# The first MLP product of a diffusion backbone by seven block products for eight

## The chip, the cores and the metric

The kernel runs on one core of a Trainium2 chip. Time is device microseconds of one execution; the number that counts is the median of several. Engine names are those of the profile: PE is TensorE (PEld its weight loads), DVE is VectorE, ACT is ScalarE, POOL is GpSimd, and SP is SyncE, which here only issues DMAs. A name with a q (SPq) is the queue of instructions of that engine. Each engine works its own queue off in order, so an instruction that waits holds up what stands behind it in that queue.

## The reference, cut to what matters

The kernel computes one layer of a hybrid backbone for 512 latent and 128 context tokens (640 in all, D = 1024), in float32. Ahead of the MLP lie an input projection, four token mixers (pooling, Fourier, RWKV-7, gated linear attention), a gated merge and an output projection. The part that the change is about:

```python
h = _rmsnorm(xf, p['norm2_g']) * (1.0 + sc2) + sh2
ff = jnp.einsum('blf,fd->bld', jnp.square(jax.nn.relu(jnp.einsum('bld,df->blf', h, p['mlp_w1']))), p['mlp_w2'])
xf = xf + g2 * ff
```

`mlp_w1` is 1024 x 4096 and `mlp_w2` 4096 x 1024. A final RMSNorm follows.

## The kernel before, in words

Every float32 matrix is split into two parts, a rounded high part (`fp32r`) and the rest. A product is then three products: high by high, high by low, low by high. The split of a weight tile is `load` (L249): a DMA of 128x512 numbers into one of three `wr` buffers (`fetch`, L238 to L242), a cast on ACT (L246) and a subtraction on DVE (L247).

Up to some 180 us the program loads the inputs, makes the modulation vectors from `ada_w` (`araw`, `acc`: DVE), and starts the input projection (`proj`, L368). Then come the two RWKV halves (`hp` = 0 and 1, from L686 on). Each needs masks made by POOL: `G.affine_select` on the tiles `ab` and `sl` (L780, 24 of them for each half), after which SP writes `ab` to DRAM as `adr` (L785) and reads it back. Between these dependent pieces PE does tiles of the input projection, which need only weights. From 521 us on come the linear attention, the gated merge and the output projection (L1240), then the MLP.

The order of the instructions on each engine is not the order of the source. A scheduler sets it: each engine gets what it believes ready, by priority (`tc.high_priority` raises it), and the order is then fixed. Ordering between engines is by semaphores.

The MLP works in four groups of 1024 hidden features. `hidden` (L1349 to L1361) makes 128 features by 320 tokens (half of the 640, `HN`): eight k-tiles by three terms, 24 matmuls of 320 columns (L1354), then the squared ReLU and the split into `fh` and `fl`. A group has 16 of these, 384 matmuls; the four together have 1536. The group then multiplies by its rows of `mlp_w2`, 240 matmuls of 512 columns (L1400), and adds the result to the residual `xf`, which stays in the fast memory of the core. The last half of the last group is L1420, with the final norm behind it. The normalised input is transposed by PE (`transposed`, L1319 to L1332) into `nh` and `nl`; that of the last 128 tokens is done inside the first `hidden` tiles.

Of the kernel before, what the change touches and what calls it, by code (L numbers as in the profile page):

```python
# [10 lines left out]
F32 = mybir.dt.float32  # L11
# [8 lines left out]
P = 128  # L20
# [45 lines left out]
def laid_out(x):  # L66
# [6 lines left out]
        "t_w1": blocks(x["mlp_w1"][0], range(0, FF, P), P),  # L73
# [63 lines left out]
def backbone(ctx, tc, a, y_prompt, y_sample, out_rwkv, out_gla):  # L137
# [484 lines left out]

    def split_into(y, j, src):
        S.copy(y[0][:, j, :], src)
        V.tensor_tensor(y[1][:, j, :], src, f32(y[0][:, j, :]), ALU.subtract)
# [60 lines left out]
    for hp in range(2):  # L686
# [221 lines left out]
        for step in range(8):  # L908
            live = [(0, 0, step), (1, 1, 2 + step)] + ([(2, 0, 8 + step), (3, 1, step)] if step < 2 else [])
# [139 lines left out]
    for n in range(7):  # L1049
        p = 64 >> n  # L1050
# [225 lines left out]
    nh = h2.tile([P, KT, NT], F32R, name="nh")  # L1276
    nl = h2.tile([P, KT, NT], F32R, name="nl")
# [16 lines left out]
    def projected(i, hf, acc, t):  # L1294
# [7 lines left out]
        S.activation(t[:, bs], xf[i][:, bs], AF.Square, accum_out=ss[:, 2 * i + hf : 2 * i + hf + 1])  # L1302

# [14 lines left out]

    def transposed(i, t):  # L1319
        c = i // 4  # L1320
        sl_ = slice(i * P, i * P + P)
        for k4 in range(2):
# [4 lines left out]
            for k in range(4):  # L1327
                kk = k4 * 4 + k
                S.activation(tm[:, k], pt[:, k * P : k * P + P], AF.Identity, scale=s2[:, kk, c : c + 1], bias=b2[:, kk, c : c + 1])
            ks = slice(k4 * 4, k4 * 4 + 4)  # L1330
            S.copy(nh[:, ks, sl_], tm)
            V.tensor_tensor(nl[:, ks, sl_], tm, f32(nh[:, ks, sl_]), ALU.subtract)  # L1332
# [14 lines left out]
    with tc.tile_pool(name="mlp", bufs=1, reuse_waits="tile") as mp, \  # L1347
            tc.tile_pool(name="pf2", bufs=5, space=PSUM, reuse_waits="tile") as pf2:
        def hidden(w, h, l, b):  # L1349
            pt = pbank()  # L1350
            bs = slice(b * HN, b * HN + HN)
            for k in range(KT):
                for n, (wk, m) in enumerate(((w[0], nh), (w[0], nl), (w[1], nh))):
                    PE.matmul(pt[:, :HN], lhsT=wk[:, k, :], rhs=m[:, k, bs], start=k == 0 and n == 0,  # L1354
                              stop=k == KT - 1 and n == 2)
            with hi():
                rl = mp.tile([P, HN], F32, name="rl", tag="rl", bufs=3)
                S.activation(rl, pt[:, :HN], AF.Relu)  # L1358
                V.tensor_tensor(rl, rl, pt[:, :HN], ALU.mult)  # L1359
                S.copy(h[:, bs], rl)  # L1360
                V.tensor_tensor(l[:, bs], rl, f32(h[:, bs]), ALU.subtract)  # L1361

        g2b = mp.tile([P, 2, D], F32, name="g2b")
        gf = mp.tile([P, D], F32, name="gf")
        NG = 4
        for g in range(NG):
            ws, fh, fl = [], [], []
            order = [(f, b) for f in range(8) for b in range(2)]
            if g == 0:
                order[:4] = [(0, 0), (1, 0), (0, 1), (1, 1)]  # L1370
            for f, b in order:
                if b == 0:
                    ws.append(load(a["t_w1"][g * 8 + f]))
                    fh.append(mp.tile([P, NT], F32R, name="fh", tag="fh", bufs=11))
                    fl.append(mp.tile([P, NT], F32R, name="fl", tag="fl", bufs=11))
                elif f == 0 and g == 0:
# [4 lines left out]
            if g == 0:  # L1381
# [81 lines left out]
```

## Time and profile before

| what | value |
|---|---|
| median of 3 runs | 1233.39 us (1231.15 to 1239.44) |
| the profiled execution | 1242.74 us, of which the span of instructions is 1241.0 us |
| mean granted clock in the profiled execution | 0.971 |
| PE busy | 1194.1 us, 96% |
| DVE busy / ACT busy / POOL busy | 734.0 / 500.5 / 61.8 us |
| moved by DMA | 147.41 MB, mean 119 GB/s |
| chain that ended last | PE 43%, of it L1354 18% and L1400 15% |

The page of the profile cuts the span into 40 slices of 31 us and gives for each the busy share of every engine in tenths, the granted TensorE clock, the busy share of the core's 16 DMA engines and the GB/s moved. The tables of stretches give the same for any piece of the span in numbers. Matmuls are pipelined, so the mean length of one (0.31 us) is longer than the time from one to the next; what counts is the length of a run of them divided by their number. The chain that ended last goes back from the last instruction, at each step to what released it. Idle time of an engine is put down to what ended it.

### The profile page before, as it was taken

How to read it: one execution, taken by the hardware profiler on the slowest of the kernel's cores; microseconds unless marked ns; L12 is line 12 of the kernel's file. 1: busy time of each engine (PE TensorE's matmuls, PEld its weight loads, DVE VectorE, ACT ScalarE, POOL GpSimd, SP SyncE). 2: the span in 40 equal slices, each digit the busy share in tenths (PEclk: the TensorE clock that was granted, in tenths of full speed). 3: DMA queues.
4: the chain of work that ended last, by engine and by line, in shares of the span. 5: the costliest groups of instructions: out<-in, count | busy, mean ns of one | idle time of the engine just before them, and what ended most of it. 6: DMA issues, size and time to landing. Idle time of an engine off the chain costs nothing.

```text
span 1241.0 us, 19640 instructions
## 1 busy us (share of the span) xinstructions
PE 1194.1 (96%) x7556; PEld 1032.8 (83%) x7556; DVE 734.0 (59%) x1458; ACT 500.5 (40%) x1024; POOL 61.8 (5%) x98
## 2 busy tenths in 40 slices
PE   7999999999998999998999989999999999999997
PEld 2778997889878798796578978998899899889985
DVE  4798767565479383446978746542453444245456
ACT  4732226542376522268535324532133124213432
POOL 0000001400114200200000000000000000000000
PEclk9999899799899699999999989999999999999998
DMA  9557652234214243153465550322222222222222
GB/s 353 207 173 256 219 182 79 74 97 118 84 48 123 59 124 101 58 172 99 150 216 159 190 197 28 100 69 83 70 78 76 79 74 75 79 78 76 69 93 85
DMA packets 85971, 147.41 MB, mean 119 GB/s; under 512 B 21693, under 2 KB 26206, under 8 KB 85878
## 3 DMA queue, kind: packets, MB, share of 16 engines
q1 hardware_dynamic: 85878, 146.16, 37.1%
q8 instruction: 59, 0.97, 0.3%
q14 instruction: 34, 0.28, 0.1%
HBM read 123.17 MB, written 22.95 MB: 118 GB/s over the span
## 4 chain that ended last, share of the span: by engine, by line
PE 43%; DMA 3%; DVE 3%; ACT 2%; issue 1%; DVEq 0%; ACTq 0%
PE pf L1354 18%; PE pf L1400 15%; PE po L1240 4%; PE pf L1420 2%; DMA wr<-in_t_out_dram 2%; PE px L1077 2%; DMA wr<-in_t_in_dram 1%; PE pt L368 1%; DVE acc L309 1%; DVE wl L247 0%; ACT eqm L1073 0%; PE pf L1325 0%; PE px L1151 0%; DVE gate L1202 0%; DMA mg<-mscr 0%
## 5 line engine op out<-in xcount | busy, mean ns | idle before, releaser
L247 DVE TENSOR_TENSOR wl<-wr,wh 128x512 fp32r<-128x512 f32 x222 | 151.4, 695 | 208.3 <-ACT wh L246 201.8
L246 ACT CAST wh<-wr 128x512 fp32r<-128x512 f32 x222 | 133.5, 618 | 345.3 <-PE pf L1400 139.1
L368 PE MATMUL pt<-xl,wh 128*128 128x320 f32 x816 | 202.0, 323 | 0.0
L368 PE MATMUL pt<-xh,wh 128*128 128x320 f32 x816 | 201.5, 324 | 0.2 <-DVE grow L337 0.2
L368 PE MATMUL pt<-xh,wl 128*128 128x320 f32 x816 | 198.1, 320 | 0.0
L1354 PE MATMUL pf<-nh,wl 128*128 128x320 f32 x512 | 158.1, 309 | 0.0
L1354 PE MATMUL pf<-nl,wh 128*128 128x320 f32 x512 | 157.9, 308 | 0.0
L1354 PE MATMUL pf<-nh,wh 128*128 128x320 f32 x512 | 157.8, 309 | 0.0
L368 PEld LDWEIGHTS pt<-xh,wh 128*128 128x128 f32 x816 | 140.1, 192 | 8.8 <-issue 4.0
L368 PEld LDWEIGHTS pt<-xl,wh 128*128 128x128 f32 x816 | 140.4, 192 | 7.7 <-issue 4.1
L368 PEld LDWEIGHTS pt<-xh,wl 128*128 128x128 f32 x816 | 139.9, 192 | 5.3 <-issue 2.2
L1400 PE MATMUL pf<-wl,fh 128*128 128x512 f32 x280 | 109.0, 389 | 0.0
L1400 PE MATMUL pf<-wh,fh 128*128 128x512 f32 x280 | 109.0, 389 | 0.0
L1400 PE MATMUL pf<-wh,fl 128*128 128x512 f32 x280 | 108.9, 389 | 0.0
L1354 PEld LDWEIGHTS pf<-nl,wh 128*128 128x128 f32 x512 | 96.0, 188 | 0.2
L1354 PEld LDWEIGHTS pf<-nh,wh 128*128 128x128 f32 x512 | 96.0, 188 | 0.1
L1354 PEld LDWEIGHTS pf<-nh,wl 128*128 128x128 f32 x512 | 96.0, 188 | 0.0
L309 DVE SCALAR_TENSOR_TENSOR acc<-araw,sc,acc 128x512 f32<-128x512 f32 x112 | 78.4, 744 | 12.5 <-DMA araw<-in_t_ada_dram 12.4
L1400 PEld LDWEIGHTS pf<-wh,fl 128*128 128x128 f32 x280 | 52.6, 188 | 11.0
L1400 PEld LDWEIGHTS pf<-wh,fh 128*128 128x128 f32 x280 | 52.5, 188 | 10.8
L1400 PEld LDWEIGHTS pf<-wl,fh 128*128 128x128 f32 x280 | 52.6, 188 | 10.8
L1359 DVE TENSOR_TENSOR rl<-rl,pf 128x320 f32<-128x320 f32 x64 | 30.9, 483 | 39.0 <-ACT rl L1358 39.0
(538 smaller groups left out, 1773.5 us busy)
## 6 DMA issues: line engine op xcount, KB each, us to landing
wr<-in_t_w_dram SPq DMA_DIRECT2D x128, 256.0 KB, 2.9
wr<-in_t_in_dram SPq DMA_DIRECT2D x102, 256.0 KB, 3.5
araw<-in_t_ada_dram SPq DMA_DIRECT2D x64, 256.0 KB, 3.7
adaw<-in_t_ada_dram SPq DMA_DIRECT2D x16, 512.0 KB, 9.3
mscr<-gate SPq DMA_DIRECT2D x24, 320.0 KB, 4.0
mg<-mscr SPq DMA_DIRECT2D x24, 320.0 KB, 4.0
uscr<-mg SPq DMA_DIRECT2D x15, 320.0 KB, 2.9
wr<-in_t_branch_dram SPq DMA_DIRECT2D x32, 128.0 KB, 2.2
```

What stands on the lines that cost most here:

```text
L246: S.copy(wh, raw)
L247: V.tensor_tensor(wl, raw, f32(wh), ALU.subtract)
L309: V.scalar_tensor_tensor(acc[j], raw, w, acc[j], ALU.mult, ALU.add)
L368: PE.matmul(pt[:, b, :HN], lhsT=w, rhs=m[:, b * HN : b * HN + HN], start=start and n == 0, stop=stop and n == 2)
L1077: PE.matmul(pt, lhsT=ek[:, ts_], rhs=em[:, :, ts_], start=True, stop=True)
L1240: PE.matmul(acc, lhsT=m[k][:, sl_], rhs=W[k, hf][w][:, 0, :], start=k == 0 and n == 0, stop=k == KT - 1 and n == 2)
L1354: PE.matmul(pt[:, :HN], lhsT=wk[:, k, :], rhs=m[:, k, bs], start=k == 0 and n == 0, stop=k == KT - 1 and n == 2)
L1359: V.tensor_tensor(rl, rl, pt[:, :HN], ALU.mult)
L1400: PE.matmul(acc[i], lhsT=m[k][:, ts_], rhs=w[:, kk, :], start=k == 0 and n == 0, stop=k == 7 and n == 2)
L1420: PE.matmul(acc, lhsT=m[k][:, ts_], rhs=ws[k][w][:, 0, :], start=k == 0 and n == 0, stop=k == 7 and n == 2)
```

## The change

The first MLP product is done on 2x2 blocks of both factors, with seven block products for eight (Strassen's scheme in Winograd's form). The input is cut by k (two halves of 512) and by tokens (two halves of 320), the weight by k and by 128 features: `t_w1` is stored in blocks of 512 rows by 128 features, 16 pairs of feature tiles. For each pair `pair_steps` does seven products of 12 matmuls of 320 columns (84 for a pair, 1344 in all) and forms the four results by additions on DVE and ACT from three banks.

Four of the seven products need sums of weight blocks. They are made in DRAM, in 16 buffers `wsum` of 1 MB (four sums for each of four groups): POOL issues 16 copying DMAs (DRAM to DRAM, `begin`) and 16 adding ones (`add`, which add their source onto the buffer). In the source `chore` places them in the RWKV loop. The sums of input blocks are made by `block_sums` on DVE and ACT after the last transposition. The residual goes to DRAM (`xres`) and comes back in the last group; `xf` collects the MLP output instead. The hidden tiles `fh` and `fl` have 8 buffers for 11.

```diff
-        "t_w1": blocks(x["mlp_w1"][0], range(0, FF, P), P),
+        "t_w1": np.ascontiguousarray(blocks(x["mlp_w1"][0], range(0, FF, P), P).reshape(16, 2, P, 2, 512).transpose(3, 1, 0, 2, 4)),
...
+    wsum = [[dpool.tile([4, P, 512], F32, name=f"wsum{n}_{g}") for g in range(4)] for n in range(4)]
+    w1b = a["t_w1"]
+    def sum_steps():
+        def rows(t):
+            return t.rearrange("j p c -> (j p) c")
+        def begin(n, g):
+            src = w1b[(0, 0, 1, 1)[n], (0, 1, 1, 0)[n], 4 * g : 4 * g + 4]
+            return lambda: nc.gpsimd.dma_start(out=rows(wsum[n][g]), in_=rows(src))
+        def add(n, g):
+            src = (w1b[0, 1, 4 * g : 4 * g + 4], w1b[1, 1, 4 * g : 4 * g + 4], wsum[0][g], wsum[2][g])[n]
+            return lambda: nc.gpsimd.dma_start(out=rows(wsum[n][g]), in_=rows(src), accum_op=ALU.add, max_dma_last_dim=8192)
+        steps = [begin(n, 0) for n in range(4)]
+        for g in range(4):
+            for n in range(4):
+                steps.append(add(n, g))
+                if g < 3:
+                    steps.append(begin(n, g + 1))
+        return steps
+    chores = sum_steps()
+    def chore(n):
+        for _ in range(min(n, len(chores))):
+            chores.pop(0)()
     def split_into(y, j, src):
...
         for step in range(8):
+            chore(2)
...
     for n in range(7):
+        chore(1)
...
-    nh = h2.tile([P, KT, NT], F32R, name="nh")
-    nl = h2.tile([P, KT, NT], F32R, name="nl")
+    nh = h2.tile([P, KT, HN], F32R, name="nh")
+    nl = h2.tile([P, KT, HN], F32R, name="nl")
+    xres = [dpool.tile([P, D], F32, name=f"xres{i}") for i in range(5)]
...
+    nf = op.tile([P, KT, HN], F32, name="nf")
...
+        if hf == 1:
+            nc.sync.dma_start(out=xres[i], in_=xf[i])
...
+    def block_sums(pool):
+        a21, a22 = nf[:, 0:4], nf[:, 4:8]
+        r = {"11": (nh[:, 0:4], nl[:, 0:4]), "12": (nh[:, 4:8], nl[:, 4:8])}
+        (h11, l11), (h12, l12) = (tuple(f32(t) for t in r[n]) for n in ("11", "12"))
+        def put(name, s):
+            h, l = (pool.tile([P, 4, HN], F32R, name=f"{n}{name}") for n in ("sh", "sl"))
+            S.copy(h, s)
+            V.tensor_tensor(l, s, f32(h), ALU.subtract)
+            r[name] = (h, l)
+        put("22", a22)
+        V.tensor_tensor(a22, a22, a21, ALU.subtract)
+        V.tensor_tensor(a21, h11, a21, ALU.subtract)
+        V.tensor_tensor(a21, a21, l11, ALU.add)
+        put("22-21", a22)
+        put("11-21", a21)
+        V.scalar_tensor_tensor(a21, a22, -1.0, h11, ALU.mult, ALU.subtract)
+        V.tensor_tensor(a21, a21, l11, ALU.subtract)
+        put("21-22-11", a21)
+        V.scalar_tensor_tensor(a21, a21, -1.0, h12, ALU.mult, ALU.subtract)
+        V.tensor_tensor(a21, a21, l12, ALU.subtract)
+        put("22-21+11-12", a21)
+        return r
...
     with tc.tile_pool(name="mlp", bufs=1, reuse_waits="tile") as mp, \
             tc.tile_pool(name="pf2", bufs=5, space=PSUM, reuse_waits="tile") as pf2:
-        def hidden(w, h, l, b):
-            pt = pbank()
-            bs = slice(b * HN, b * HN + HN)
-            for k in range(KT):
-                for n, (wk, m) in enumerate(((w[0], nh), (w[0], nl), (w[1], nh))):
-                    PE.matmul(pt[:, :HN], lhsT=wk[:, k, :], rhs=m[:, k, bs], start=k == 0 and n == 0,
-                              stop=k == KT - 1 and n == 2)
+        spool = ExitStack()
+        A = {"11": (nh[:, 0:4], nl[:, 0:4]), "12": (nh[:, 4:8], nl[:, 4:8])}
+        def product(pt, m, src, first):
             with hi():
-                rl = mp.tile([P, HN], F32, name="rl", tag="rl", bufs=3)
-                S.activation(rl, pt[:, :HN], AF.Relu)
-                V.tensor_tensor(rl, rl, pt[:, :HN], ALU.mult)
-                S.copy(h[:, bs], rl)
-                V.tensor_tensor(l[:, bs], rl, f32(h[:, bs]), ALU.subtract)
-
-        g2b = mp.tile([P, 2, D], F32, name="g2b")
-        gf = mp.tile([P, D], F32, name="gf")
+                wh, wl = load(src.unsqueeze(1), mp, "st", 4)
+                wh, wl = wh[:, 0], wl[:, 0]
+            mh_, ml_ = A[m]
+            for k in range(4):
+                ks = slice(k * P, k * P + P)
+                for n, (w, x) in enumerate(((wh, mh_), (wh, ml_), (wl, mh_))):
+                    PE.matmul(pt[:, :HN], lhsT=w[:, ks], rhs=x[:, k, :], start=first and k == 0 and n == 0,
...
+        def pair_steps(j):
...
+            p1, u2, u3 = st(), st(), st()
+            product(ba, "11", b11, True)
+            with hi():
+                S.copy(p1, ba)
+            yield
+            product(bb, "21-22-11", wsum[2][g][q], True)
+            with hi():
+                V.tensor_tensor(u2, p1, bb, ALU.add)
+            yield
+            product(ba, "12", b21, False)
+            with hi():
+                rl = st()
+                S.activation(rl, ba, AF.Relu)
+                S.activation(rl, rl, AF.Square)
+                parts_of(rl, h0, l0, t0)
+            product(bc, "22-21", wsum[0][g][q], True)
+            product(bb, "11-21", wsum[1][g][q], False)
+            with hi():
+                V.tensor_tensor(u3, p1, bb, ALU.add)
+                c = st()
+                V.tensor_tensor(c, u3, bc, ALU.add)
+                S.activation(c, c, AF.Relu, scale=-1.0)
+                S.activation(c, c, AF.Square)
+                parts_of(c, h1, l1, t1)
+            yield
+            product(bb, "22", wsum[3][g][q], False)
+            with hi():
+                V.tensor_tensor(p1, p1, bb, ALU.add)
+                V.scalar_tensor_tensor(p1, p1, 0.0, p1, ALU.max, ALU.mult)
+                parts_of(p1, h0, l0, t1)
+            yield
+            product(bc, "22-21+11-12", b22, False)
+            with hi():
+                V.tensor_tensor(u2, u2, bc, ALU.add)
+                V.scalar_tensor_tensor(u2, u2, 0.0, u2, ALU.min, ALU.mult)
+                parts_of(u2, h1, l1, t0)
+            yield
...
+            fh, fl = [], []
+            before_ = None
+            for j in range(4):
+                now = pair_steps(4 * g + j)
+                next(now)
+                if g == 0 and j == 0:
                     with hi():
                         transposed(4, before)
+                        A.update(block_sums(spool.enter_context(tc.tile_pool(name="spool", bufs=1, reuse_waits="tile"))))
                     ops.close()
-                hidden(ws[f], fh[f], fl[f], b)
-            if g == 0:
+                if before_:
+                    next(before_)
+                next(now)
+                if before_:
+                    next(before_)
+                next(now)
+                before_ = now
+            next(before_)
+            next(before_)
...
+            if g == NG - 1:
+                spool.close()
+                h2pool.close()
+                w2pool = ExitStack()
+                w2p = w2pool.enter_context(tc.tile_pool(name="w2pool", bufs=1, side="right", reuse_waits="tile"))
+                g2b = w2p.tile([P, 2, D], F32, name="g2b")
+                gf = w2p.tile([P, D], F32, name="gf")
...
+                for i in range(5):
+                    xr = w2p.tile([P, D], F32, name="xr", tag="xr", bufs=2)
+                    nc.sync.dma_start(out=xr, in_=xres[i])
+                    V.tensor_tensor(xf[i], g2b[:, i // 4, :], xf[i], ALU.mult)
+                    V.tensor_tensor(xf[i], xf[i], xr, ALU.add)
             def residual(i, hf, acc):
                 cs_ = slice(hf * 512, hf * 512 + 512)
-                t = mp.tile([P, 512], F32, name="mt", tag="mt", bufs=3)
+                if g == 0:
+                    return S.copy(xf[i][:, cs_], acc)
+                if g < NG - 1:
+                    return V.tensor_tensor(xf[i][:, cs_], xf[i][:, cs_], acc, ALU.add)
+                t = w2p.tile([P, 512], F32, name="mt", tag="mt", bufs=3)
                 V.tensor_tensor(t, g2b[:, i // 4, cs_], acc, ALU.mult)
                 V.tensor_tensor(xf[i][:, cs_], xf[i][:, cs_], t, ALU.add)
 
@@ -1404,8 +1557,7 @@
...
```

What the change does to the order on the engines is seen at three places.

First, POOL, from its two first memsets to the masks of the first RWKV half (`ab`, `sl`). Before:

```order
L377 MEMSET pw 128x256
L381 MEMSET pos 64x1152
L852 MEMSET xc 64x2x64 x2
L698 MEMSET TT 128x1280
L780 ISA
L780 AFFINE_SELECT ab<-ab 64x512
L780 AFFINE_SELECT sl<-sl 64x512
```

Now (`wsum_0`: sums of the first group; rows of L633 copy, rows of L637 add and wait for an earlier transfer):

```order
L377 MEMSET pw 128x256
L381 MEMSET pos 64x1152
L633 DMA wsum_0_1459<-in_t_w_dram 16x16384
L633 DMA wsum_0_1463<-in_t_w_dram 16x16384
...
L637 DMA wsum_3_1470<-wsum_3_1462 128x2048
L637 DMA wsum_3_1474<-wsum_3_1470 128x2048
L883 MEMSET xc 64x2x64 x2
L729 MEMSET TT 128x1280
L811 ISA
L811 AFFINE_SELECT ab<-ab 64x512
```

All 32 transfers stand in one block behind the second memset and ahead of everything that POOL does for the RWKV halves, 28 of them in the rows left out.

Second, PE, where the MLP begins (`ot` is a normalised tile that is transposed, `pf` a bank). Before, the last two transpositions stand between matmuls of `hidden`, 384 of which follow one another:

```order
L1325 MATMUL pf_7985<-cst,ot 128x128 x4
L1354 MATMUL pf_8034<-nh,wh 128x320
...
L1325 MATMUL pf_8106<-cst,ot 128x128 x4
L1354 MATMUL pf_8076<-nh,wl 128x320
...
L1325 MATMUL pf_8118<-cst,ot 128x128 x4
L1354 MATMUL pf_8076<-nh,wl 128x320
```

Now 24 matmuls of the first pair stand ahead of the last transpositions and 12 of the second pair behind them; the next one needs the block sum `sh21-22-11`:

```order
L1390 MATMUL pf_8050<-cst,ot 128x128 x4
L1435 MATMUL pf_8083<-nh,sth 128x320
...
L1390 MATMUL pf_8112<-cst,ot 128x128 x4
L1390 MATMUL pf_8122<-cst,ot 128x128 x4
L1435 MATMUL pf_8248<-nh,sth 128x320
...
L1435 MATMUL pf_8084<-sh21-22-11_8152,sth 128x320
L1435 MATMUL pf_8085<-sh22-21_8142,sth 128x320
```

Third, DVE at that place (`nf` holds the second half of the tokens, `sl...` the low part of a sum, 1280 numbers in a row; `stl` is a weight split). The rows between the last normalisation and the first result of a pair:

```order
L1346 TENSOR_SCALAR ot<-xf_7678,rs_8062 128x512 x2
L1365 TENSOR_TENSOR sl_8136<-nf,sh_8135 128x1280
L247 TENSOR_TENSOR stl<-wr,sth 128x512
L1369 TENSOR_TENSOR nf<-nf 128x1280
L1370 TENSOR_TENSOR nf<-nh,nf 128x1280
L1365 TENSOR_TENSOR sl22-21_8143<-nf,sh22-21_8142 128x1280
L1371 TENSOR_TENSOR nf<-nf,nl 128x1280
L1365 TENSOR_TENSOR sl11-21_8147<-nf,sh11-21_8146 128x1280
L1374 SCALAR_TENSOR_TENSOR nf<-nf,nh 128x1280
L1375 TENSOR_TENSOR nf<-nf,nl 128x1280
L1365 TENSOR_TENSOR sl21-22-11_8153<-nf,sh21-22-11_8152 128x1280
```

None of these stood there before. The sum that PE waits for is complete with the row of L1375 and a cast on ACT behind it.

## Rows read from the trace of the kernel before

**Rows 1.** The page, part 2: busy tenths in 40 slices of 31 us.

```profile
PE   7999999999998999998999989999999999999997
...
DVE  4798767565479383446978746542453444245456
...
DMA  9557652234214243153465550322222222222222
```

**Rows 2.** The chain that ended last: start us, duration us, engine and line.

```profile
790.96 0.63 PE pf L1325 x4
...
792.49 51.67 PE pf L1354 x352
844.16 54.45 PE pf L1400 x240
...
1176.48 27.24 PE pf L1400 x120
```

**Rows 3.** Table of stretches: busy us of each engine, clock, DMA share, GB/s.

```profile
core 0: us, PE busy (x) PEld busy (x) DVE busy (x) ACT busy (x) POOL busy (x), PEclk, DMA share, GB/s
0.00:214.00 214.00, 199.29 (x1150) 163.98 (x1150) 158.07 (x300) 90.36 (x158) 6.26 (x13) 0.98 0.63 213
10.00:20.00 10.00, 10.00 (x22) 2.94 (x21) 5.26 (x8) 6.59 (x12) 0.00 (x0) 1.00 1.02 409
228.00:232.00 4.00, 3.76 (x26) 3.22 (x26) 1.49 (x4) 2.83 (x6) 2.06 (x3) 0.85 0.02 5
232.00:236.00 4.00, 4.00 (x15) 3.17 (x14) 0.76 (x2) 2.32 (x4) 2.60 (x4) 0.50 0.00 0
240.00:244.00 4.00, 4.00 (x18) 3.44 (x18) 1.26 (x4) 1.96 (x5) 0.46 (x2) 0.50 0.06 10
```

**Rows 4.** POOL in order of time: start us, duration us, instruction, idle before.

```profile
1.17 1.06 POOL L381 MEMSET pos<- 64x1152 f32 x1
54.56 0.45 POOL L852 MEMSET xc<- 64x128 f32 x2 [52.33 <-PE px L444]
...
209.45 0.67 POOL L780 TENSOR_SCALAR_AFFINE_SELECT ab<-ab 64x512 f32<-64x512 f32 x1 [118.41 <-ACT ab L776]
...
240.12 0.41 POOL L780 TENSOR_SCALAR_AFFINE_SELECT sl<-sl 64x256 f32<-64x256 f32 x1
```

**Rows 5.** SP queue in order of time: DMAs issued, 218 to 244 us.

```profile
222.01 1.90 SPq L785 DMA_DIRECT2D adr<-ab  x3
...
226.07 14.31 SPq L785 DMA_DIRECT2D adr<-ab  x4
243.46 0.35 SPq L241 DMA_DIRECT2D wr<-in_t_in_dram  x1
```

**Rows 6.** Waits of SP, 200 to 260 us: total us, times, longest.

```profile
SPq L785 <- POOL ab L780: 16.7, 4, 10.7
```

**Rows 7.** The page, part 6: DMA issues, KB each, median us to landing.

```profile
wr<-in_t_w_dram SPq DMA_DIRECT2D x128, 256.0 KB, 2.9
```

**Rows 8.** VectorE in order of time, second hidden tile of the MLP.

```profile
799.71 0.48 DVE L1359 TENSOR_TENSOR rl<-rl,pf 128x320 f32<-128x320 f32 x1
800.11 0.68 DVE L247 TENSOR_TENSOR wl<-wr,wh 128x512 fp32r<-128x512 f32 x1
800.71 0.49 DVE L1361 TENSOR_TENSOR fl<-rl,fh 128x320 fp32r<-128x320 f32 x1
```

**Rows 9.** PE in order of time, first matmul of the MLP.

```profile
786.10 0.39 PE L1354 MATMUL pf<-nh,wh 128*128 128x320 f32 x1
```

**Rows 10.** ScalarE in order of time, start of the MLP.

```profile
793.86 1.19 ACT L1329 ACTIVATE tm<-pf,b,s 128x128 f32<-128x128 f32 x3
...
795.93 0.46 ACT L1360 CAST fh<-rl 128x320 fp32r<-128x320 f32 x1
798.44 0.62 ACT L246 CAST wh<-wr 128x512 fp32r<-128x512 f32 x1 [2.05 <-PE pf L1354]
```

More of the change, by code (lines that the diff above doesn't have):

```diff
@@ L1328, in transposed @@
                 kk = k4 * 4 + k
-                S.activation(tm[:, k], pt[:, k * P : k * P + P], AF.Identity, scale=s2[:, kk, c : c + 1], bias=b2[:, kk, c : c + 1])
+                m = min(max(HN - i * P, 0), P)
+                if m > 0:
+                    S.activation(tm[:, k, :m], pt[:, k * P : k * P + m], AF.Identity, scale=s2[:, kk, c : c + 1],
+                                 bias=b2[:, kk, c : c + 1])
+                if m < P:
+                    S.activation(nf[:, kk, i * P + m - HN : i * P + P - HN], pt[:, k * P + m : k * P + P], AF.Identity,
+                                 scale=s2[:, kk, c : c + 1], bias=b2[:, kk, c : c + 1])
             ks = slice(k4 * 4, k4 * 4 + 4)
-            S.copy(nh[:, ks, sl_], tm)
-            V.tensor_tensor(nl[:, ks, sl_], tm, f32(nh[:, ks, sl_]), ALU.subtract)
+            m = min(max(HN - i * P, 0), P)
+            if m > 0:
+                S.copy(nh[:, ks, i * P : i * P + m], tm[:, :, :m])
+                V.tensor_tensor(nl[:, ks, i * P : i * P + m], tm[:, :, :m], f32(nh[:, ks, i * P : i * P + m]), ALU.subtract)
     for i in range(4):
@@ L1363, in backbone @@
-        g2b = mp.tile([P, 2, D], F32, name="g2b")
-        gf = mp.tile([P, D], F32, name="gf")
+        spool = ExitStack()
+        A = {"11": (nh[:, 0:4], nl[:, 0:4]), "12": (nh[:, 4:8], nl[:, 4:8])}
+        def product(pt, m, src, first):
+            with hi():
+                wh, wl = load(src.unsqueeze(1), mp, "st", 4)
[5 more added lines that the diff above has]
+                    PE.matmul(pt[:, :HN], lhsT=w[:, ks], rhs=x[:, k, :], start=first and k == 0 and n == 0,
+                              stop=k == 3 and n == 2, skip_group_check=True)
@@ new lines, in st, with parts_of @@
+        def st():
+            return mp.tile([P, HN], F32, name="sums", tag="sums", bufs=6)
+        def parts_of(x, h, l, bs):
+            S.copy(h[:, bs], x)
+            V.tensor_tensor(l[:, bs], x, f32(h[:, bs]), ALU.subtract)
+        def pair_steps(j):
+            g, q = j // 4, j % 4
+            f0, f1 = 2 * (j % 4), 2 * (j % 4) + 1
+            b11, b12, b21, b22 = (w1b[kh, fh_, j] for kh in range(2) for fh_ in range(2))
+            ba, bb, bc = pbank(), pf2.tile([P, 512], F32, name="pf2", tag="pf2"), pf2.tile([P, 512], F32, name="pf2", tag="pf2")
+            ba, bb, bc = (t[:, :HN] for t in (ba, bb, bc))
+            H, L = fh, fl
+            for _ in range(2):
+                H.append(mp.tile([P, NT], F32R, name="fh", tag="fh", bufs=8))
+                L.append(mp.tile([P, NT], F32R, name="fl", tag="fl", bufs=8))
+            h0, l0, h1, l1 = H[f0], L[f0], H[f1], L[f1]
+            p1, u2, u3 = st(), st(), st()
[35 more added lines that the diff above has]
+            yield
@@ L1365, in backbone @@
         NG = 4
         for g in range(NG):
-            ws, fh, fl = [], [], []
-            order = [(f, b) for f in range(8) for b in range(2)]
-            if g == 0:
[L1370 to L1376, printed above, removed]
+            fh, fl = [], []
@@ L1404, in backbone @@
                         residual(i, hf, acc[i])
-        h2pool.close()
-        with tc.tile_pool(name="w2pool", bufs=1, side="right", reuse_waits="tile") as w2p:
+        with w2pool:
             ws = [load(a["t_w2"][(NG - 1) * 4 + k // 2, 1, :, k % 2 : k % 2 + 1], w2p, f"w2{k}", 1) for k in range(8)]
```

2 lines of the change are left out of this document (1 added, 1 removed).

## The prediction

> **What bounds the kernel now.** I read the slices of the page first, then the chain of waits, then tables of stretches, and last POOL and the SP queue in order of time. The slices say that PE is the busy engine nearly everywhere, while the DMA engines are full only in the first two slices and far from it from the twentieth on [rows 1]. The chain shows the MLP as nothing but PE: runs of L1354 and L1400 without a gap from 792.5 us on [rows 2]. There 352 matmuls of 320 columns take 51.67 us, 0.147 us each. So in the MLP a matmul less is time less. The first 214 us are another stage: PE is busy too, but the 16 DMA engines carry a mean share of 0.63, and from 10 to 20 us 1.02 at 409 GB/s, which is their full rate here [rows 3].
>
> **What goes.** 1536 - 1344 = 192 matmuls of L1354: 192 x 0.147 = **-28.2 us**. All of it lies on the path, since the new matmuls have the same shape.
>
> **The weight sums.** In the source they lie in the RWKV loop, but in the order of POOL all 32 transfers stand behind the memset of `pos`, which ends at 2.2 us [rows 4]. The first four wait for nothing and start there; each adding one waits for an earlier transfer, so POOL is held until nearly all have landed. Behind them stand the memset of `xc`, which POOL did at 54.6 us, and the 24 masks of the first RWKV half, from 209.5 to 240.5 us [rows 4]. Behind the masks waits SP with `adr` (L785), and behind `adr` in SP's queue the next weight tiles `wr`. Rows show what that costs: SP waited 16.7 us for the masks, in four waits [rows 6], the next `wr` went out only at 243.5 us [rows 5], and PE fell to the lower clock level (0.50 of 2.4 GHz) from 232 to 244 us, 15 matmuls in 4 us where it had done 26 [rows 3]. So nothing may be late on POOL beyond about 214 us (SP's first `adr` is at 222.0 us, and 12 masks of 0.67 us come ahead of it).
>
> How long do the transfers take? Before there is no copy from DRAM to DRAM and no adding DMA, so I bound them. One MB at the full 409 GB/s is 2.56 us [rows 3]. From below: each of the 32 costs one such pass, 82 us. From above: every read and write of DRAM costs a pass, two for a copy and three for an addition, 16 x 2 + 16 x 3 = 80 passes, 205 us. The nearest row, the full-rate stretch, holds reads of DRAM only; by it a copy is one pass and an addition, which reads two operands, two: 123 us. The writes to the same memory will cost something more; I take the middle of 123 and 205, 164 us.
>
> The DMA engines are busy 0.63 x 214 = 135 us before POOL's deadline and free 79 us. 164 us of new work into 79 us of room leaves 85 us over. That holds for an even share of the engines: both run for 270 us, then 29 us of transfers are left, POOL is free at 299 us, 85 us late. If the new transfers take 60% they are done at 273 us, but the old loads have had 109 us, which by 0.63 a us is where they were at 173 us: 100 us late. I take **+95 us**. The delay is not won back: after it everything runs at its old pace, since PE has no slack to make up [rows 1].
>
> What the Trainium skill says of this: "DMA: Bandwidth & Descriptors", section Issuing engines are not separate DMA queues, has all queues run on the same 16 DMA engines, so that a second queue saves only issue time. No run here has shown a second queue yet. The same page, Latency and other measured facts, gives about 214 GB/s in each direction for copies between HBM tensors. An estimate from that figure: 4.9 us for a copied MB and half as much again for an added one, 196 us in all, and the delay would be 117 us for my 95. Nothing below is taken from these sentences.
>
> **The start of the MLP.** The next PE row behind 36 matmuls needs the sum `21-22-11`. The evacuation of the last transposition ends at 793.86 + 1.19 = 795.05 us [rows 10]. DVE starts a 320-wide operation and the next one 0.40 us later, a 512-wide one 0.60 us [rows 8]: 1.04 ns a column, 1.40 us for 1280 columns. ACT's casts, 0.46 and 0.62 us [rows 10], give 1.26 us. The chain by the order of DVE: cast 1.26, low part 1.40, a weight split 0.60, L1369 and L1370 2.80, low part 1.40, L1371 1.40, cast 1.26 and low part 1.40, L1374 and L1375 2.80, cast 1.26: 15.6 us, to 810.6 us. PE's twelve matmuls behind the transposition are done by then for 14 us or more. Ahead of it, 24 matmuls from 786.1 us [rows 9] end at 789.6 us, and the transposition comes at 791.0 us [rows 2]. Together PE stands for about **+18 us**, where before it had other `hidden` tiles. From below, casts beside DVE's work could save 3 us; from above, a stall of 16 us can drop PE to the lower clock level as in rows 3, 12 us at half speed, +6 us.
>
> **The products.** A pair is 84 x 0.147 = 12.3 us of PE. DVE has 7 splits and 11 operations of 320 columns, 7 x 0.60 + 11 x 0.40 = 8.6 us; ACT 7 x 0.62 + 9 x 0.46 = 8.5 us [rows 8, 10]. Both fit. The raw weights are tighter: one 256 KB tile for every 1.76 us of PE, from three buffers. A buffer's round is 2.9 us to land [rows 7], 0.62 for the cast, 0.68 for the subtraction and some 0.3 us to issue, 4.5 / 3 = 1.5 us; with one foreign operation ahead on each engine (0.46 and 0.48) 5.4 / 3 = 1.8 us, 0.04 us more than PE needs, 112 x 0.04 = 5 us. And a bank that is added to (`22` onto `11-21`) gives DVE only one product of 1.76 us to read it. Between 0 and 10 us; I take **+4 us**.
>
> **At nothing**, with their cover: the copies of the residual (10 DVE operations of 1024 columns, 11 us by the same rate) lie beside the last group's L1400, 27.2 us of PE [rows 2]; without that cover they cost up to 11 us. Five stores `xres` take SP 0.3 us each in a stage in which it waits for buffers; at most 2 us. Two hidden buffers fewer bind nothing, since a group has eight and PE reads them in order. The residual's addition is one operation for two.
>
> **Sum:** 95 - 28 + 18 + 4 = +89 us. The profiled execution took 1242.7 us, 9.3 above the median of the runs shown; in its conditions 1332 us, and against the median of 1233.4 us **1322 us**.
>
> **The rivals.**
> *The new transfers are served first and the old loads stand still*, with all 80 passes: POOL is free at 207 us, but the program is then where it was at 2 us, a delay of 205 us: 1233 + 205 - 6 = 1432 us. For it: the copies are 16 rows of 64 KB against rows of 2 KB in the weight tiles. Against it: nothing in the rows shows that long rows go first. By a rule of the Trainium skill ("DMA: Bandwidth & Descriptors", Queues, rings and completion order) an engine goes round its queues packet by packet, which would favour the longer packets; no run here shows it. Chance 0.12.
> *The transfers are hidden.* If each of the 32 costs one pass (82 us) and they fall into the 79 us that are free, POOL is late by 3 us and the old loads run as before: 1233 + 3 - 28 + 18 + 4 = 1230 us. It decides at some 80 us of transfers. For it: a share of 0.63. Against it: the first 31 us are full [rows 1], and an addition reads twice. Chance 0.10.
> *Hidden, and the start of the MLP covered*: with a stall of 5 us for 18, since casts and DVE overlap better than I chain them, 1217 us, faster. Chance 0.11.
> That the change does not do what it says is half true already: its transfers don't lie in the RWKV loop. The seven products for eight are there.
>
> **How the numbers follow.** Forecast 0.67, with a range of its own from 1267 us (delay 40, transfers of 119 us at an even share) to 1392 us (delay 165: 205 us of transfers with 75% of the engines are done at 273 us, the old loads at 108). From 1230 to 1425 us the range takes in the hidden case and most of the first rival; outside are 0.11 below and about 0.07 above. About 1%, 12 us, is what a measurement of this kernel can tell from no change. Slower by more than that: 0.67 + 0.12 = 0.79; within it 0.10; faster 0.11.
>
> **What would show it.** In the slices DMA at 9 through the first eight or nine. POOL's first mask near 300 us for 209.5. `wr` landing in 5 us or more in the first stage, with ACT's casts waiting for it. A PE gap of 15 to 18 us ahead of the first product with a block sum, then some 49 us for a group's 336 matmuls. It is wrong if the first mask still comes near 210 us, or if the transfers take under 80 us; or, in the other direction, if a group of products takes 56 us as before.

## The result, and the profile after

Four runs of each on one chip: 1358.3 us with the change (1356.3 to 1362.7), 1236.4 before (1231.2 to 1240.5), ratio 1.099 with a 95% interval of 1.094 to 1.105. The change makes the kernel 122 us slower; 89 were forecast. The two profiled executions stand only 114 us apart (spans 1355.1 and 1241.0), because that of the kernel before was a slow one, 6 us above its median (its clock in the MLP was 1.00, so stages of the MLP can be compared).

Part 2 of the page after (busy tenths in 40 slices, 34 us each; PEclk is the granted clock) answers to [rows 1]:

```profile
PE   2143699999999999999989998985999999999997
...
PEclk9566699899999995999999999987999999999998
DMA  9999947762333132331634564332423523523562
```

The loss is at the left edge: through five slices the DMA engines are full, PE is at a tenth to six tenths and its clock falls with it. From the sixth slice on the row of PE looks like the one before. Stretches of that edge, in the columns of [rows 3]:

```profile
0.00:50.00 50.00, 6.83 (x10) 2.74 (x10) 7.92 (x29) 9.16 (x17) 11.75 (x22) 0.77 0.98 306
50.00:100.00 50.00, 19.93 (x24) 2.20 (x24) 4.09 (x15) 3.29 (x4) 7.21 (x11) 0.65 1.03 283
100.00:150.00 50.00, 19.93 (x50) 7.91 (x50) 6.16 (x9) 7.19 (x10) 3.32 (x4) 0.59 1.00 270
150.00:200.00 50.00, 43.59 (x263) 37.68 (x263) 36.07 (x64) 25.59 (x46) 1.21 (x3) 0.93 0.66 208
```

In 150 us PE did 84 matmuls, where [rows 3] have 1150 in 214 us. What it waited for, 0 to 200 us (total us, times, longest):

```profile
PE px L287 <- DMA adaw<-in_t_ada_dram: 65.1, 8, 34.8
PE px L404 <- DMA pos<-in_k_pos_dram: 15.8, 1, 15.8
```

`adaw` are the first weights of the head, loaded by SP. Part 6 of the pages (KB each, median us to landing), before and then after:

```profile
adaw<-in_t_ada_dram SPq DMA_DIRECT2D x16, 512.0 KB, 9.3
```

```profile
adaw<-in_t_ada_dram SPq DMA_DIRECT2D x16, 512.0 KB, 57.1
wsum<-in_t_w_dram POOLq DMA_DIRECT2D x8, 1024.0 KB, 27.8
wsum<-wsum POOLq DMA_DIRECT2D x8, 1024.0 KB, 19.1
```

The same tile takes six times as long, beside the transfers of POOL. Part 3 says what the 32 transfers used in all (packets, MB, share of 16 engines' span), and POOL in order of time when they ended, which answers to [rows 4]:

```profile
q0 software_dynamic: 2816, 33.56, 9.3%
```

```profile
2.18 2.19 POOL L633 DMA_DIRECT2D wsum<-in_t_w_dram  x4
...
152.97 0.81 POOL L637 DMA_DIRECT2D wsum<-wsum  x1 [17.50 <-DMA wsum<-wsum]
175.51 0.45 POOL L883 MEMSET xc<- 64x128 f32 x2 [21.72 <-ACT xh L452]
210.82 1.17 POOL L729 MEMSET TT<- 128x1280 f32 x1 [34.86 <-DMA yscr<-ft]
330.58 0.66 POOL L811 TENSOR_SCALAR_AFFINE_SELECT ab<-ab 64x512 f32<-64x512 f32 x1 [118.58 <-ACT ab L807]
```

0.093 x 1355.1 = **126 us** of all engines. Summed over the packets by their size, 42 us of it are the 16 copies (packets of 64 KB) and 84 the 16 adds (8 KB). The last adding DMA goes out at 153.0 us and lands 10.9 us later, at 163.9. Up to there the engines were busy all the time (share 1.00), 164 us; 126 went to the transfers and 38, or **23%**, to the loads of the program. Before, at a share of 0.87 over its first 44 us, the program had had 38 us of the engines by 44 us. So at 164 us it stood where it had stood at 44, 120 us late. Its first mask is 121 us late (330.6 for 209.5). The delay is not won back: against the profiled execution of the second experiment below, the changed kernel without its transfers, it is 124 us at the first mask (206.95 us there) and 125 at the first product of the out projection (803.4 for 678.8 us). The masks waited for ACT, not for POOL, which was free of its transfers at 154 us.

**The MLP nets nothing.** From its chain (start us, us, engine and line), which answers to [rows 2]:

```profile
888.58 10.91 PE po L1273 x48
...
902.10 4.04 DMA wr<-in_t_w_dram
...
927.59 1.27 ACT sh21-22-11_8152 L1364
...
928.90 38.25 PE pf L1435 x239
...
977.33 53.52 PE pf L1553 x236
1030.85 29.15 PE pf L1435 x199
```

From one group's down product (the second product of the MLP, L1553) to the next it is 104.05 us (977.33 to 1081.38) where the kernel before had 110.78: 6.7 us a group, 27 in all. But PE waits 14.1 us for `sh21-22-11`, and from 920 to 935 us its clock is at 0.50. From the end of the out projection to the end of the program the two traces have 455.5 and 455.6 us.

### The profile page after: what moved, and what is told of

It is laid out like the page before. It is cut to its first block, busy times and chain, and to the rows that moved or that the text cites. A ratio compares the mean times of both kernels' runs of the same rounds, so it can differ in the third digit from the quotient of the medians.

```text
span 1355.1 us, 19661 instructions
## 1 busy us (share of the span) xinstructions
PE 1187.7 (88%) x7364; PEld 1006.1 (74%) x7364; DVE 792.9 (59%) x1532; ACT 545.0 (40%) x1107; POOL 84.3 (6%) x130
## 5 line engine op out<-in xcount | busy, mean ns | idle before, releaser
L247 DVE TENSOR_TENSOR wl<-wr,wh 128x512 fp32r<-128x512 f32 x158 | 107.4, 697 | 194.9 <-ACT wh L246 188.5
L246 ACT CAST wh<-wr 128x512 fp32r<-128x512 f32 x158 | 94.7, 618 | 305.5 <-PE pt L368 110.3
L1553 PE MATMUL pf<-wl,fh 128*128 128x512 f32 x280 | 109.0, 389 | 0.0
L1553 PE MATMUL pf<-wh,fl 128*128 128x512 f32 x280 | 109.0, 389 | 0.0
L1553 PE MATMUL pf<-wh,fh 128*128 128x512 f32 x280 | 109.0, 389 | 0.0
L247 DVE TENSOR_TENSOR stl<-wr,sth 128x512 fp32r<-128x512 f32 x112 | 77.1, 691 | 46.1 <-ACT sth L246 45.3
L246 ACT CAST sth<-wr 128x512 fp32r<-128x512 f32 x112 | 69.1, 619 | 82.4 <-PE pf L1435 58.7
L309 DVE SCALAR_TENSOR_TENSOR acc<-araw,sc,acc 128x512 f32<-128x512 f32 x112 | 78.5, 746 | 12.0 <-DMA araw<-in_t_ada_dram 11.9
L287 PE MATMUL px<-adaw,scw 128*8 128x512 f32 x32 | 26.7, 987 | 65.1 <-DMA adaw<-in_t_ada_dram 65.1
L287 PEld LDWEIGHTS px<-adaw,scw 128*8 128x8 f32 x32 | 3.0, 113 | 87.9 <-issue 46.0
L1553 PEld LDWEIGHTS pf<-wh,fh 128*128 128x128 f32 x280 | 52.6, 188 | 10.8
L1553 PEld LDWEIGHTS pf<-wh,fl 128*128 128x128 f32 x280 | 52.6, 188 | 10.8
L1553 PEld LDWEIGHTS pf<-wl,fh 128*128 128x128 f32 x280 | 52.6, 188 | 10.6
L1435 PE MATMUL pf<-nh,sth 128*128 128x320 f32 x128 | 40.5, 316 | 1.3 <-ACT nf L1399 0.7
L1442 ACT CAST fh<-sums 128x320 fp32r<-128x320 f32 x64 | 29.4, 459 | 30.3 <-DVE sums L1491 16.6
L1435 PE MATMUL pf<-nh,stl 128*128 128x320 f32 x128 | 40.2, 314 | 0.2 <-DVE stl L247 0.2
## 6 DMA issues: line engine op xcount, KB each, us to landing
adaw<-in_t_ada_dram SPq DMA_DIRECT2D x16, 512.0 KB, 57.1
wsum<-in_t_w_dram POOLq DMA_DIRECT2D x8, 1024.0 KB, 27.8
wsum<-wsum POOLq DMA_DIRECT2D x8, 1024.0 KB, 19.1
```

The costliest lines, as they stand in the source:

```text
L246: S.copy(wh, raw)
L247: V.tensor_tensor(wl, raw, f32(wh), ALU.subtract)
L287: PE.matmul(pt[0:8, :], lhsT=c[:, 4 * part : 4 * part + 8, k + j], rhs=w[:, j], start=part == 1 and k + j == 0 and n == 0, stop=part == 0 ...
L309: V.scalar_tensor_tensor(acc[j], raw, w, acc[j], ALU.mult, ALU.add)
L1435: PE.matmul(pt[:, :HN], lhsT=w[:, ks], rhs=x[:, k, :], start=first and k == 0 and n == 0, stop=k == 3 and n == 2, skip_group_check=True)
L1442: S.copy(h[:, bs], x)
```

## Experiments

Two theories stood open. **Starvation:** the transfers take the engines from the loads of the head, wherever POOL stands. **My own:** POOL is held, at an even share of the engines.

**1. The transfers alone.** The 32 transfers put into the kernel before, into tensors that nobody reads.

```diff
+    wsum = [[dpool.tile([2, P, 1024], F32, name=f"wsum{n}_{g}") for g in range(4)] for n in range(4)]
...
         for step in range(8):
+            chore(2)
```

> The kernel before with the 16 copies and 16 adding transfers of 1 MB each put at the same place on POOL's queue; what they write is read by nobody, and the MLP stays as it was. Theory (the transfers take the DMA engines from the loads of the head, and the MLP part of the change nets nothing): the whole loss comes back, 1340 to 1360 us, with the first mask near 330 us and the adaw loads landing after some 57 us in place of 9. Rival (the loss is partly the MLP's, the transfers alone cost what my forecast gave them, 80 to 100 us): 1315 to 1335.

1351.9 us (1348.8 to 1354.0), ratio 1.097 (1.092 to 1.102). First mask at 324.3 us, `adaw` landing after 56.8 us. The whole loss is the transfers': they alone cost as much as the change.

**2. The change without them**; the products read plain blocks of weights where they read sums.

```diff
-    chores = sum_steps()
+    chores = []
...
-            product(bb, "21-22-11", wsum[2][g][q], True)
+            product(bb, "21-22-11", b21, True)
...
```

> The changed kernel without any of the 32 transfers; where a product reads a summed block of weights it reads a plain block of the same size, so the result is not the reference's and the instructions on the engines are the same. Theory (the MLP part nets nothing: 27 us of matmuls won, 25 us lost at its start, 2 at its end): 1230 to 1242 us. Rival (the MLP part is a gain of 10 to 20 us that the late head covers up): 1215 to 1226 us.

1229.2 us for 1231.8 of the kernel before, ratio 0.999 (0.996 to 1.002). Seven products for eight are worth nothing as written.

**3. Rows of 2 KB, at the same place.**

```diff
-            return lambda: nc.gpsimd.dma_start(out=rows(wsum[n][g]), in_=rows(src))
+            return lambda: nc.gpsimd.dma_start(out=rows(wsum[n][g]), in_=rows(src), max_dma_last_dim=2048)
...
-            return lambda: nc.gpsimd.dma_start(out=rows(wsum[n][g]), in_=rows(src), accum_op=ALU.add, max_dma_last_dim=8192)
+            return lambda: nc.gpsimd.dma_start(out=rows(wsum[n][g]), in_=rows(src), accum_op=ALU.add, max_dma_last_dim=2048)
```

> The changed kernel with all 32 transfers cut into rows of 2 KB, as the loads of SP's queue have them, in place of rows of 64 KB (copies) and 8 KB (adds); bytes and order are the same. Theory (the transfers won three quarters of the engines because their rows are longer): with an even share the loads of 0 to 214 us, 135 us of the engines, go beside 126 us of transfers until about 252 us, and the first mask comes 40 to 55 us late in place of 121: 1275 to 1295 us. Rival (the share does not hang on the length of the rows): 1345 to 1370 us, or more if short rows cost the engines more.

1322.3 us (ratio 1.074): 36 us come back, about half of what the theory gave. Parts 3 and 6 of its page:

```profile
q0 software_dynamic: 12800, 33.56, 10.2%
```

```profile
adaw<-in_t_ada_dram SPq DMA_DIRECT2D x16, 512.0 KB, 20.2
```

`adaw` lands in 20.2 us for 57.1, so the length of the rows does decide the share. The transfers now use 0.102 x 1319.2 = 135 us (in the trace the adds go in packets of 2 KB, the copies in packets of 4 KB), and the last one lands at 214.6 us. At a share of 1.04 the engines were busy 223 us by then, so the loads got 88, or 39%. Before, 88 us were reached at 122 us (share 0.72 up to there): 92 us late, and the first mask is 84 late (293.2 us).

This run also decides between the two theories for this place: POOL was held by its adds longer than in the change, until 204.7 us for 153.8, and still the first mask came 37 us earlier (293.2 for 330.6). What counts is what the loads get, not how long POOL is held. My expectation erred in taking the demand of the head as even, 0.63 a us: it wants 0.84 in its first 50 us.

**4. The same transfers spread over the RWKV steps**, in the trace from 255 to 547 us, and **5. the same with rows of 2 KB.**

```diff
                 xn = new_x(step + 1)
+                with tc.issue_after(getattr(mark[0], "ins", mark[0])):
+                    chore(3)
```

`mark[0]` is the last copy of `xc`.

> The changed kernel with the same 32 transfers, but each group of three held on POOL's queue behind the copies of xc of one RWKV step, from about 290 to 530 us, where the share of the DMA engines was 0.24 to 0.37. Theory (the loss came from the place: the head needs its loads at once, these stages do not): 1230 to 1250 us. Rival (126 us of transfers starve the loads wherever they run, or POOL, held by its adds, is late with the masks of the second pair of heads): 1270 to 1330 us.

> The kernel with the transfers spread over the RWKV steps (1272 us), with all rows cut to 2 KB. Theory (there the loads of the in-projection were held back by long rows, 29.6 us of ACT waiting for wr): they get an even share, and 10 to 25 us come back: 1247 to 1262 us. Rival (what is lost there is POOL waiting in its adds while xc and the masks are due; short rows make each transfer land later, 30.7 for 22.6 us where all came at once): 1272 to 1290 us.

1272.1 us (1.032), and 1264.4 (1.025) with short rows. The head is as before (first mask at 208.8 us), so 86 us of the loss were the place; but the 40 us left over the kernel before are a miss of the theory, and short rows gave back 8, less than it said. Waits of all engines in the kernel with long rows, 250 to 680 us:

```profile
POOL wsum L637 <- DMA wsum<-wsum: 53.1, 4, 16.4
...
ACT wh L246 <- DMA wr<-in_t_in_dram: 33.7, 7, 14.9
...
PE pt L368 <- ACT gate L1220: 14.1, 2, 7.6
...
PE px L804 <- ACT big L790: 10.3, 1, 10.3
...
PE pxc L948 <- POOL xc L879: 9.5, 3, 7.6
```

By these waits both theories are at work here. Loads are held back: ACT stands for `wr` in its casts, and PE for what lies behind them on ACT. And POOL is held in its adds while PE wants `xc`. With short rows PE's wait for `xc` grows to 17.7 us and that for `gate` shrinks to 4.6. How the 40 us divide between the two was not tried.

**6. The transfers late**: the first group's behind a one-column copy of `xf[4]`, the others by twos beside the products of the group before; and **7. with a shorter start of the MLP**.

```diff
+        ins = G.tensor_copy(tok, src[:, 0:1])
+        with tc.issue_after(getattr(ins, "ins", ins)):
+            chore(n)
...
+    chores_behind(8, xf[4], late)
...
                 parts_of(rl, h0, l0, t0)
+            if chores:
+                chores_behind(2, f32(h0), late)
```

> The changed kernel with the transfers put late: the eight of the first group held behind a one-column copy of xf[4] on POOL (about 725 us), those of each later group two by two behind a one-column copy from each of the four pairs of the group before. POOL has nothing else to do there. Theory (the loss was only the place of the transfers, and what was lost with them spread over the RWKV steps was loads held back there and POOL waiting in its adds): 1226 to 1240 us, as without transfers. Rival (rows of 64 KB hold back the loads of 2 KB rows also at a DMA share of 0.24, and the MLP's three buffers of weights run dry): 1245 to 1275 us.

> The kernel with the transfers put late, and a shorter start of the MLP: the block sums in two pieces of columns, the first 192 (of the tokens 320 to 511) ahead of the last transposition, the other 128 behind it, and the products with blocks 11 and 12 of the first two pairs (48 matmuls, 7 us) ahead of the first product with a sum. Theory (the chain of the sums is what the start waits for): 8 to 15 us under the kernel with late transfers alone, 1214 to 1224 us, faster than the kernel before. Rival (the splits of the weights on DVE fill the same time, or the two pieces cost as much again in shorter instructions): within 4 us of the kernel with late transfers alone.

1305.5 us (1.058): slower, as the rival had it, and by 30 us more than its range. POOL has nothing else to do here, and the stages that lose are the up stages, the first products of the MLP, with a DMA share of their own of 0.43 to 0.52. Waits of ACT and of SP, 700 to 1310 us:

```profile
ACT sth L246 <- DMA wr<-wsum: 68.9, 17, 7.9
...
ACT sth L246 <- DMA wr<-in_t_w_dram: 25.8, 15, 4.0
```

```profile
SPq L241 <- DMA wsum<-wsum: 30.1, 1, 30.1
```

A group takes 125 to 127 us for 104. SP's one wait for a sum that was not ready, 30.1 us, lies beside the out projection (732 to 762 us); the seventh kernel has no such wait and still takes 126 to 128 us a group, so there the loss is starved loads. The seventh kernel has 1288.3 us, 17 less but far from its 1214 to 1224, and not for the reason given: PE still waited 11.9 us for the first sum, and of the 21 us between the two profiled executions 13 are the out projection, which ended at 775 for 788 us.

**8. No block sums.** The kernel without transfers, with plain halves in place of the sums.

```diff
+        for name, k in (("22", "11"), ("22-21", "12"), ...):
+            r[name] = r[k]
+        return r
         put("22", a22)
```

> The kernel without transfers, less the block sums: the products read plain halves of nh and nl where they read the five sums, so the result is not the reference's, the products are as many and as large, and the 22 instructions of block_sums on ACT and DVE are gone. Theory (25 us are lost at the start of the MLP because PE waits for that chain, 14.1 us in the trace of the change, and runs some 10 us after it at the lower clock): 15 to 20 us under the kernel without transfers (1229), 1209 to 1214 us. Rival (the splits of the first weights on DVE and their loads are what the start waits for, and the chain only lies beside them): 1222 to 1230 us.

1210.5 us, ratio 0.980 (0.973 to 0.987), 18.6 under the second kernel, as the theory had it. The two ran on different chips; by their ratios to the kernel before (0.999 and 0.980) the difference is 24 us, and so it is in the two traces: from the end of the out projection to the first down product it is 77.5 us with the sums and 53.7 without. The sums at the start of the MLP cost that much, 19 to 24 us, and about 1210 is what the change can reach if its sums cost nothing.

**9. and 10. The quiet places**: the first group's transfers one by one behind RWKV steps, the others in the down products, whose DMA share without transfers was 0.26 to 0.30 (0.43 to 0.52 in the up stages); rows of 2 KB, and rows of 64 and 8 KB.

```diff
+                if step in ((1, 2, 3, 4), (1, 2, 3, 5))[hp]:
+                    with tc.issue_after(getattr(mark[0], "ins", mark[0])):
+                        chore(1)
...
             next(before_)
             next(before_)
+            if chores:
+                chores_behind(8, f32(fh[7]), late)
```

> The kernel with the shorter start of the MLP, and the transfers in rows of 2 KB in the places where the trace without transfers has the least use of the DMA engines and POOL nothing to do: the four copies of the first group one behind each RWKV step of the first pair of heads, its four adds one behind each step of the second pair, and the eight transfers of each later group behind the last hidden block of the group before, that is in the down product, where the share was 0.26 to 0.30 (0.43 to 0.52 in the up stages where the last placement had them). Theory (what a transfer costs is decided by the loads that run beside it): little is lost, 17 us under the kernel without transfers less some us, 1213 to 1230 us, at or under the kernel before. Rival (the loads of the weights are held back wherever 32 MB more pass the engines): 1245 to 1280 us.

> The same kernel with the rows of the change, 64 KB in the copies and 8 KB in the adds. Theory (long rows take three quarters of the engines while a transfer is under way, rows of 2 KB half): 8 to 25 us over the same kernel with short rows. Rival (at this share there is room beside either, and long rows cost the engines less in all, 126 us for 135): within 4 us of it.

1231.4 us with short rows, ratio 0.998 (0.995 to 1.002), and 1270.3 with long ones, 1.030 (1.024 to 1.036). Place and order are the same; 39 us hang on the length of the rows, more than either theory had. The same three stretches of both, short rows first:

```profile
870.00:920.00 50.00, 50.00 (x266) 44.54 (x266) 18.57 (x32) 20.99 (x42) 2.01 (x2) 1.00 0.76 186
...
970.00:1020.00 50.00, 50.00 (x257) 43.84 (x256) 22.23 (x37) 15.07 (x29) 2.02 (x2) 1.00 0.82 195
...
1070.00:1120.00 50.00, 48.44 (x236) 41.43 (x235) 18.65 (x30) 11.85 (x21) 2.01 (x2) 1.00 0.84 203
```

```profile
870.00:920.00 50.00, 41.65 (x173) 33.44 (x172) 8.80 (x13) 12.55 (x22) 1.61 (x2) 0.90 0.70 167
...
970.00:1020.00 50.00, 41.33 (x171) 33.22 (x170) 12.00 (x21) 6.84 (x12) 5.72 (x9) 0.90 0.85 228
...
1070.00:1120.00 50.00, 42.90 (x223) 36.99 (x221) 17.94 (x34) 13.89 (x29) 4.91 (x8) 0.97 0.79 222
```

At nearly the same DMA share PE is all but full beside short rows and stands 7 to 9 us in each 50 beside long ones. From one down product to the next it is 104 us with short rows and 115 to 116 with long ones, which in three groups makes up most of the 39 us. With short rows the time is a little above the theory's range: the 17 us of the seventh kernel did not come along. PE's wait for the first sum was 11.9 us here too, behind 7 us of matmuls put ahead. DVE showed why: from 782 to 805 us it worked almost without a pause through both pieces, interleaved, and the sum that PE wanted first was the fourth of five.

**11. The sums in the order in which they are wanted**, in one piece again, and the product with `11-21` ahead of the one with `22-21`.

```diff
-        put("22", a22)
-        V.tensor_tensor(a22, a22, a21, ALU.subtract)
         V.tensor_tensor(a21, h11, a21, ALU.subtract)
         V.tensor_tensor(a21, a21, l11, ALU.add)
+        put("11-21", a21)
+        V.scalar_tensor_tensor(a21, a21, -1.0, a22, ALU.mult, ALU.subtract)
+        put("21-22-11", a21)
+        put("22", a22)
...
```

> The kernel with the transfers in rows of 2 KB at the quiet places, with the block sums in one piece again and written in the order in which the products want them: 11-21 from the half of nf that is transposed first, then 21-22-11 from it by one instruction, 22, 22-21 and the last; the products of the first two pairs with 11 and 12 stay ahead. In the trace of that kernel PE waited 11.9 us for 21-22-11, while DVE worked without a pause from 782 to 805 us, because the two pieces ran interleaved. Theory (the wait is the count of DVE instructions ahead of the first sum that a product reads, not the work of all five): five of 1.4 to 1.5 us and one copy of 1.3 us stand there now behind the last transposition, 9 us for some 19, the wait falls to 1 to 4 us and the time by 7 to 12 us, to 1217 to 1225 us. Rival (DVE is full at this place, and what the first product gains the next ones lose): within 4 us of 1231.

1224.6 us, ratio to the kernel before 0.993 (0.989 to 0.997): 6.7 us under the ninth kernel, at the upper edge of the theory, though the intervals of the two ratios overlap. PE's waits from 740 us on:

```profile
PE pf L1438 <- ACT sh21-22-11_8118 L1367: 7.2, 1, 7.2
PE pf L1393 <- DVE ot L1349: 4.2, 1, 4.2
```

The wait fell from 11.9 to 7.2, not to 1 to 4: the copy of `22` came before the one of `11-21` on ACT, and two splits of weights and a `fl` lay between the DVE operations. This version is the one that beats the kernel before, by 0.7% (0.3 to 1.1): clear of the noise, and small.

## Why the prediction came out as it did

A slower kernel was forecast, and 1358 us lie in the range that was given. That is in part luck: the largest term, 95 us for some 121, came as near as it did because wrong inputs met, and by another way than the one forecast (see the weight sums).

*Products, -28.2 us:* right. 6.7 us a group, 27 in all, at the 0.147 us a matmul of [rows 2].

*Start of the MLP, +18 us:* mis-sized. Of the chain, the first sum came out at 928.9 us, 16.3 behind the end of the last transposition's evacuation (912.55), for 15.6 worked out. The start cost 25 us (131.35 us from 899.5 to 1030.85, for 113.1 before less the 6.7 won). The pieces not in the term: a load and a split of weights ahead of the last normalization (4 us of `wr` in the chain), and the clock at 0.50 from 920 to 935, which I had as an upper bound only. The eighth kernel, without the chain and so without that fall of the clock, gives 19 to 24 for the two together.

*Three buffers of raw weights, +4 us:* not found. A group is won 6.7 of 7.05 us, so at most 0.3 a group. Some 2 us were lost at the end instead, where I had put nothing: `g2b` and the copies of the residual come into the chain beside the last products.

*Weight sums, +95 us:* the place was read rightly from the order of POOL, and its price is the greatest part of the error, 121 us at the first mask. Three of the inputs failed and their errors partly met. The work was taken as 164 us and is 126, close to the bound of 123 with one pass for a copy and two for an addition, and so in its parts: 42 us for the copies (41 in the bound), 84 for the adds (82). The share was taken as even, or 60% at most, and is 77 to 23. The demand of the head was taken as even, 0.63 a us, and is 0.87 in its first 44 us. With 126 us at an even share the same sum gives 47 us, with 164 us at this share about 150 (done at 213 us, the loads with 49 us, which before had by 64). And the step that followed, POOL held until 299 us and late for its masks, did not happen at all: POOL was free at 154 us, and in the third kernel it was held longer and the masks came earlier. The delay came through SP's loads, which the second way of the sum, loads held back at a share of 60%, had in it; 65.1 us of it stand in one row, PE waiting for `adaw`. By the waits shown, POOL being held did cost time elsewhere, in the fourth and fifth kernels.

*The rivals:* "new transfers first, the old loads stand still" had the mechanism more nearly than my forecast, with the work of all 80 passes, which was too much: with 126 us of work it gives 126 us of delay. I had given it 0.12, saying that nothing in the rows showed long rows going first. The Trainium skill's rule cited there ("DMA: Bandwidth & Descriptors", Queues, rings and completion order), engines going round the queues packet by packet, agrees in its direction with what the runs showed when the rows alone were cut: 23% to 39% for the loads in the third kernel, 39 us between the ninth and tenth. The estimate of 196 us of work from the figure for copies on that page of the Trainium skill (Latency and other measured facts) does not agree with the 126 measured.
Hidden transfers (1230 us) did not come about here: the DMA slices at the start were full. The ninth kernel, with the transfers elsewhere and in short rows, has that time.

*What would show it:* DMA stood at 9 through five slices, not eight or nine; the first mask was at 330 us, not 300; in the first 170 us a `wr` took 14.4 us to land (median; 3.9 before), and ACT's casts waited for it, as said:

```profile
ACT wh L246 <- DMA wr<-in_t_in_dram: 74.1, 3, 62.4
```

The gap of PE was 14.1 us, a little under the 15 to 18, and 336 matmuls took 49.2 us in the eleventh kernel's chain, as said.

What stays open: how the share hangs on the length of the rows. By the packets of the trace the loads had 20% from 5 to 15 us, where only copies in rows of 64 KB were under way, and 21% from 127 to 145 us, with only adds in rows of 8 KB; but copies and adds differ in more than their rows. How much of the delay is PE's lower clock in the first 150 us was not tried by itself.

## What to carry to other kernels

A transfer that "nobody waits for" is charged to whoever loads beside it: take its engine time and its share, find in the trace before when the old loads had had what is left to them, and the difference is the delay (120 us for 121 measured at the first mask with long rows, 92 for 84 with short ones). Give background transfers rows no longer than those of the loads that matter, and put them where the DMA share is low and a scheduler can't move them up. Before an algorithm with fewer products is priced, price the serial chain that makes its operands at the point where the stage begins, and write it in the order in which they are wanted.

## What the runs showed of the hardware

A DRAM to DRAM copy of 1 MB cost 42 / 16 = 2.6 us of all 16 engines in rows of 64 KB, an adding transfer 84 / 16 = 5.2 us in rows of 8 KB, twice as much; in the third kernel, with the rows cut, 2.7 and 5.7 us. With long rows the loads beside them, in rows of 2 and 4 KB, were left 23% of the engines; with cut rows 39%. An adding transfer cost POOL 0.8 us to issue and landed in about the time of a copy (medians of 27.8 us and 19.1 us for the two kinds of add, 22.4 for the copies). DVE's 1280-column operations took 1.40 to 1.50 us in the chain, ACT's 1.27, for 1.40 and 1.26 worked out from the smaller rows of the kernel before.
